# ACT and DVE follow the order of the source in the mixer of a hybrid encoder layer

## The chip, the core and the metric

The kernel runs on one core of a Trainium2 chip. The metric is the time of one execution in device microseconds. Five engines work side by side, each through its own queue of instructions: TensorE (PE, matrix products), VectorE (DVE) and ScalarE (ACT) for element-wise work, GpSimd (POOL), and SyncE (SP), which starts most transfers.

## What is computed

The reference is one encoder layer on 512 tokens of width 1024. All is in float32.

```
x = x + 0.5 * swiglu(rms_norm(x, ffn1_norm), ffn1_w_gate, ffn1_w_up, ffn1_w_down)
h = rms_norm(x, mix_norm)
qkv_a, z_a, a_a, b_a, qkv_b = split(h @ w_in)
o_a = gdn_mixer(qkv_a, z_a, a_a, b_a, conv_w, a_log, dt_bias, gdn_norm_w)
o_b = dilated_mixer(qkv_b, q_norm_w, k_norm_w, rel_bias)
x = x + concat(o_a, o_b) @ w_out
x = x + 0.5 * swiglu(rms_norm(x, ffn2_norm), ffn2_w_gate, ffn2_w_up, ffn2_w_down)
x = rms_norm(x, final_norm)
```

`gdn_mixer` is a gated delta rule in both directions, with 4 heads of 128: a centred convolution of width 5 over the tokens of q, k and v, a decay per head, and per chunk of 64 tokens the inverse of a triangular matrix, followed by a scan over the chunks. `dilated_mixer` is attention with 8 heads of 64, in three patterns of window and dilation.

## The kernel before

The stages are FFN1, mixer, output projection, FFN2 and a last norm. Tokens lie on the free axis, 512 to a tile, and channels on the 128 partitions. To get float32 results from faster products, each operand is split into a high half (a rounded copy) and a low half (the rest), and each product is made of three matmuls: high by high, high (weight) by low, low (weight) by high (`mm3`).

In the mixer the input projection is cut into units of 128 output channels, named by what they make: K0 to K3 and Q0 to Q3 (keys and queries of the delta rule), V0 to V3, Z0 to Z3 (the gate of its output), and Pa, Pb, v for the attention. A unit takes two weight chunks of 128x512, and a chunk is used by twelve matmuls. A chunk (`wrw`) is loaded by SP; `split` makes its high half on ACT and `sub` its low half on DVE (`wsp`). `wnext` hands out chunks and lets the next splits be traced, one chunk ahead.

After a K, Q or V unit `conv` multiplies the result `pc` by the norm factor R on DVE (`xp`), makes the first tap on ACT and four more taps on DVE (`kT`, `qT`, `vT`). The gates (`gt`, from `ab` and `abT`) are small operations of 128x32 on DVE with a few on ACT. `gram` makes for one head the squares on ACT, the products `pkk` and `pkq` on TensorE, and from them for both directions `itr` on DVE, a product on POOL and `M` on DVE, four each. `M` of all heads goes to DRAM and comes back as `MM` in another layout; `solve` copies it on DVE and runs 31 steps (`stp`, `ZZ`) on DVE. Attention tiles are `L`, `PT` and `ou`; `otok` holds the scan's output.

What sets the order: six generators trace the mixer's work, and `interleave` picks the next piece by planned costs and due times; ORDER lists the projection units. What is so traced is then put on the engines by a scheduler, which may choose another order within an engine. In the mixer TensorE is exempt: `PEQueue` ties each matmul behind the one traced before it while `te.fixed` holds.

Of the kernel before, what the change touches and what calls it, by code (L numbers as in the profile page):

```python
# [58 lines left out]
        return self._call(self.te.transpose, *a, **k)  # L59


def interleave(streams):


    due = {i: 0.0 for i in range(len(streams))}
    need, events, t = {}, {}, 0.0
    while due:
        for i in list(need):
            if need[i] in events:
                due[i] = max(due[i], events[need.pop(i)])  # L70
        live = [i for i in due if i not in need]
        now = [i for i in live if due[i] <= t]
        if not now:
            t = min(due[i] for i in live)
            continue
        i = now[0]
        y = next(streams[i], None)
        if y is None:
            del due[i]
        elif y[0] == "set":  # L80
            events[y[1]] = t + y[2]
        elif y[0] == "need":
            need[i] = y[1]
        else:
            t += y[0]
            due[i] = t + y[1]
# [2 lines left out]
@with_exitstack  # L89
def encoder_layer(ctx, tc, xT, gu1, dn1, win, wab, wo1, wo2, gu2, dn2, cols, relb, masks, onehot, lnc, sel, out):  # L90
    nc = tc.nc
    te, ve, se, gp, sy = PEQueue(tc, nc.tensor), nc.vector, nc.scalar, nc.gpsimd, nc.sync

    const = ctx.enter_context(tc.tile_pool(name="const", bufs=1))
    xp_ = ctx.enter_context(tc.tile_pool(name="xp", bufs=1))
# [9 lines left out]
    def pfl(name):  # L105
        return ps.tile([P, T], F32, tag="fl", name=name, bufs=2)
# [16 lines left out]
    def tmp(tag, name, n=T, dt=F32, bufs=2):  # L123
        return tp.tile([P, n], dt, tag=tag, name=name, bufs=bufs)
# [30 lines left out]
    def preload():  # L155
        with ExitStack() as es:
            for i in act["silu"][-8:]:
                es.enter_context(tc.issue_after(i.ins))
            act["pre"] = se.preload_act_table_set(LE)
        act["silu"] = []  # L160
# [76 lines left out]
    def rsq(o, src, n, tag="sq"):  # L237
        a = tmp(tag, "nw")
        w = o.shape[-1]
        a = a[:, 0:w]  # L240
        lx(o, src, AF.Ln, bias=eps, scale=1.0 / n)
        lx(o, o, AF.Exp, scale=-0.5)
        se.activation(a, o, AF.Square, scale=1.0 / math.sqrt(n))
        ve.scalar_tensor_tensor(out=a, in0=src, scalar=n * EPS, in1=a, op0=ALU.add, op1=ALU.mult)
        ve.scalar_tensor_tensor(out=o, in0=a, scalar=-3.0, in1=o, op0=ALU.add, op1=ALU.mult)

    class Norm:
        def __init__(self, ccol, lone=None, fast=False):
            self.acc = tmp("ssq", "ssq", bufs=1)
            self.c, self.lone, self.fast, self.tail = ccol, lone, fast, None  # L250
# [116 lines left out]
    with ExitStack() as mctx:  # L367
        mp = mctx.enter_context(tc.tile_pool(name="mp", bufs=1, reuse_waits="tile"))

        def mt(shape, name, tag=None, dt=F32, bufs=1):  # L370
            return mp.tile(shape, dt, name=name, tag=tag or name, bufs=bufs)
# [202 lines left out]
        def silu1(t):  # L574
            with tc.issue_after(act["dexp"].ins):
                silu(t, t)
# [91 lines left out]
        def norms():  # L668
            for pr in range(4):
                yield ("need", f"pair{pr}")  # L670
                if pr == 0:
                    yield ("need", "vsilu")
                if pr:
                    yield ("need", f"split{pr - 1}")
                for isq, t, sq in pend[pr]:
                    pn = pfl("pnb")
                    te.matmul(pn, lhsT=mk[:, M_BLK:M_BLK + P], rhs=sq, start=True, stop=True)
                    yield 0.86, 0.0
                    rs = tmp("g", "rsb")
                    n = mt([P, T], "qn" if isq else "kn")  # L680
                    rsq(rs, pn, 64.0)
                    ve.scalar_tensor_tensor(out=n[:, ::-1] if isq else n, in0=t,
                                            scalar=wqk[:, 0:1] if isq else wqk[:, 1:2], in1=rs, op0=ALU.mult,
                                            op1=ALU.mult)
                    qkn[isq] = n
                yield ("set", f"norm{pr}", NRG)
# [13 lines left out]
        def post_val(h, vT):  # L700
            pt = pflip("ptr")
            for c in range(NC):
                te.transpose(out=pt[:, c * P:(c + 1) * P], in_=vT[:, c * P:(c + 1) * P], identity=ident)
            for c in range(NC):
                se.mul(vtok[:, h, c, :], pt[:, c * P:(c + 1) * P], ivn[:, h * 4 + c:h * 4 + c + 1])

        def after():
            for i in range(8):
                yield ("need", f"post{i}")
                kind, h, t = posts[i]  # L710
                if kind == "V":
                    yield ("need", "solve" if h > 1 else "gram")
                    if h == 2:
                        yield ("need", f"post{i + 1}")
                        for n in range(2):
                            gin["taps", 10 + n]()
                            silu1(posts[i + n][2])
                        preload()
                        yield ("set", "vsilu", 0.0)
                        yield 0.0, VTP  # L720
                    post_val(h, t)
                else:
                    post_v(h, t)
                yield 0.43, VTS
                if kind == "v":
                    yield ("set", f"vb{h}", VBG)
                if sum(p[0] == "V" for p in posts[:i + 1]) == 4:
                    yield ("set", "vtok", VTG)
# [61 lines left out]
        def chain():  # L790
            for h in range(NH):
                yield ("need", f"gin{h}")
                yield from gram(h)
            ve.reciprocal(t16, ivn)
            ve.tensor_tensor(out=t16, in0=t16, in1=wk, op=ALU.mult)
            ve.tensor_tensor(out=ivn, in0=ivn, in1=t16, op=ALU.add)
            ve.tensor_scalar(out=ivn, in0=ivn, scalar1=0.5, scalar2=None, op0=ALU.mult)
            yield ("set", "gram", 1.0)
            yield from solve()
            yield ("set", "solve", SVG)  # L800
            yield from levels()
# [268 lines left out]
        def fin(pr):  # L1070
            oh_[4 + pr], ol_[4 + pr] = slot(f"xh{pr}", "oh", F32R), slot(f"xl{pr}", "ol", F32R)
            split(oh_[4 + pr], ol_[4 + pr], obs[pr])
# [132 lines left out]
        def fins():  # L1205
            yield ("need", "proj")
            for pr in range(4):
                yield ("need", f"close{pr}")
                fin(pr)
                if pr == 1:  # L1210
                    yield ("set", "fin", FNG)

        ss = [fins(), chain(), after(), norms(), att(), px()]
        interleave([ss[i] for i in PRI])
        te.fixed = False
        for d in range(NKT):
            x[d] = slot(f"x{d}")
# [130 lines left out]
```

## Time and profile before

| | |
|---|---|
| median of 3 runs | 1103.24 us (1103.19 to 1105.31) |
| the profiled execution's own time | 1104.93 us |
| its span | 1103.2 us |
| TensorE busy | 1067.6 us |
| DVE busy | 614.8 us |
| ACT busy | 443.4 us |
| POOL busy | 87.0 us |

The span is the time from the first to the last recorded instruction; the execution's own time has 1.7 us around it. FFN1 lasts to about 369 us, the mixer and output projection to 729, FFN2 to 1060.

### The profile page before, as it was taken

To read this page: it belongs to the slowest core of one execution; us is meant where nothing else is said; L and a number is where in the kernel's file an instruction comes from. 1 tells how busy PE (TensorE), PEld (TensorE's weight loads), DVE (VectorE), ACT (ScalarE), POOL (GpSimd) and SP (SyncE) were. 2 spreads that over 40 slices of the span, in tenths; PEclk is the share of its full clock that TensorE was granted. 3 is DMA by queue.
4 is the path that set the end of the run, shared out by engine and by line. 5 is a ranking of instruction groups with operands and counts; after the bars stand their busy time and mean duration, and the time that the engine had idled before them with its cause. 6 is when DMAs were issued, how large, how long until landed. Compare 5 with 4: busy or idle time off the path is not lost.

```text
span 1103.2 us, 14133 instructions
## 1 busy us (share of the span) xinstructions
PE 1067.6 (97%) x5394; PEld 879.2 (80%) x5394; DVE 614.8 (56%) x1113; ACT 443.4 (40%) x812; POOL 87.0 (8%) x123
## 2 busy tenths in 40 slices
PE   9999999999999999899999988999999999999996
PEld 7888888888888777778789766778888888888886
DVE  4544444443434398898787889675444444532223
ACT  6432222232232256434666666463222222332321
POOL 3000000000111222610000010000000000001001
PEclk9999999999999999989999999999999999999998
DMA  5332222234333133445422142232233323333332
GB/s 193 96 96 96 95 96 97 95 112 148 109 121 119 35 102 101 114 120 159 90 75 94 56 160 75 68 118 83 96 99 96 103 95 105 96 87 102 89 105 77
DMA packets 53235, 112.27 MB, mean 102 GB/s; under 512 B 17984, under 2 KB 20576, under 8 KB 53168
## 3 DMA queue, kind: packets, MB, share of 16 engines
q1 hardware_dynamic: 48976, 99.50, 29.3%
q0 software_dynamic: 2896, 10.25, 2.9%
q10 hardware_dynamic: 1296, 1.63, 0.5%
q8 instruction: 42, 0.69, 0.3%
q14 instruction: 25, 0.20, 0.1%
HBM read 102.39 MB, written 8.96 MB: 101 GB/s over the span
## 4 chain that ended last, share of the span: by engine, by line
PE 81%; DVE 11%; ACT 2%; issue 2%; DMA 1%; POOL 1%; DVEq 0%; SPq 0%; ACTq 0%; POOLq 0%
PE pg L52 22%; PE pd L52 22%; PE pu L52 22%; PE pc L50 3%; PE pd L50 2%; PE pqk L50 2%; DVE wsp L226 2%; PE ps L50 2%; PE pl L50 1%; PE pov L50 1%; PE pout L52 1%; PE pT L50 1%; DVE stp L842 1%; PE pS L50 1%; DMA wrw<-in_win 1%
## 5 line engine op out<-in xcount | busy, mean ns | idle before, releaser
L178 ACT CAST whi<-wraw 128x1024 fp32r<-128x1024 f32 (+1 forms) x138 | 137.5, 999 | 425.8 <-issue 167.6
L179 DVE TENSOR_TENSOR wlo<-wraw,whi 128x1024 fp32r<-128x1024 f32 (+1 forms) x138 | 161.1, 1168 | 135.5 <-ACT whi L178 131.2
L52 PE MATMUL pd<-hh,whi 128*128 128x512 f32 (+1 forms) x374 | 141.2, 378 | 0.0
L52 PE MATMUL pd<-hh,wlo 128*128 128x512 f32 (+1 forms) x374 | 140.9, 377 | 0.0
L52 PE MATMUL pd<-hl,whi 128*128 128x512 f32 (+1 forms) x374 | 140.8, 377 | 0.0
L52 PE MATMUL pg<-xh,whi 128*128 128x512 f32 x344 | 135.2, 393 | 0.7 <-ACT whi L178 0.5
L52 PE MATMUL pg<-xl,whi 128*128 128x512 f32 x344 | 135.0, 392 | 0.3 <-DVE xl L273 0.3
L52 PE MATMUL pg<-xh,wlo 128*128 128x512 f32 x344 | 134.6, 391 | 0.0
L52 PE MATMUL pu<-xh,wlo 128*128 128x512 f32 x344 | 133.8, 389 | 0.0
L52 PE MATMUL pu<-xh,whi 128*128 128x512 f32 x344 | 133.8, 389 | 0.0
L52 PE MATMUL pu<-xl,whi 128*128 128x512 f32 x344 | 133.8, 389 | 0.0
L316 DVE TENSOR_TENSOR u<-pu,R 128x512 f32<-128x512 f32 x44 | 30.4, 691 | 129.5 <-PE pu L52 129.5
L52 PEld LDWEIGHTS pd<-hl,whi 128*128 128x128 f32 x374 | 70.3, 188 | 13.1
L52 PEld LDWEIGHTS pd<-hh,whi 128*128 128x128 f32 x374 | 70.3, 188 | 12.9
L52 PEld LDWEIGHTS pd<-hh,wlo 128*128 128x128 f32 x374 | 70.3, 188 | 12.8
L314 DVE TENSOR_TENSOR g<-pg,R 128x512 f32<-128x512 f32 x44 | 30.4, 692 | 84.7 <-PE pg L52 84.6
L52 PEld LDWEIGHTS pg<-xh,whi 128*128 128x128 f32 x344 | 65.0, 189 | 15.0 <-ACT whi L178 1.2
L52 PEld LDWEIGHTS pg<-xl,whi 128*128 128x128 f32 x344 | 64.9, 189 | 14.9 <-DVE xl L273 1.1
L52 PEld LDWEIGHTS pg<-xh,wlo 128*128 128x128 f32 x344 | 64.8, 188 | 13.9 <-issue 0.2
L229 ACT CAST wsp<-wrw 128x512 fp32r<-128x512 f32 x76 | 47.2, 621 | 71.1 <-DMA wrw<-in_win 27.6
L52 PEld LDWEIGHTS pu<-xl,whi 128*128 128x128 f32 x344 | 64.6, 188 | 13.5
L52 PEld LDWEIGHTS pu<-xh,wlo 128*128 128x128 f32 x344 | 64.6, 188 | 13.3
(296 smaller groups left out, 1692.4 us busy)
## 6 DMA issues: line engine op xcount, KB each, us to landing
wraw<-in_gu SPq DMA_DIRECT2D x84, 512.0 KB, 3.5
wraw<-in_dn SPq DMA_DIRECT2D x32, 512.0 KB, 3.5
wrw<-in_win SPq DMA_DIRECT2D x56, 256.0 KB, 2.7
wraw<-in_dn SPq DMA_DIRECT2D x16, 384.0 KB, 3.1
wrw<-in_wo SPq DMA_DIRECT2D x16, 256.0 KB, 2.6
bw<-vec_d POOLq DMA_DIRECT2D x8, 448.0 KB, 4.0
x<-in_xT SPq DMA_DIRECT2D x8, 256.0 KB, 4.8
x_d<-x SPq DMA_DIRECT2D x8, 256.0 KB, 2.0
```

Of the source, the lines that this page charges most:

```text
L50: self.last = f(*a, **k)
L52: self.last = f(*a, **k)
L178: se.copy(hi[:, s], raw[:, s])
L179: ve.tensor_tensor(out=lo[:, s], in0=raw[:, s], in1=hi.bitcast(F32)[:, s], op=ALU.subtract)
L226: ve.tensor_tensor(out=o, in0=a, in1=b.bitcast(F32), op=ALU.subtract)
L229: se.copy(hi, src)
L314: ve.tensor_tensor(out=g, in0=pg, in1=R, op=ALU.mult)
L316: ve.tensor_tensor(out=u, in0=pu, in1=R, op=ALU.mult)
L842: ve.tensor_tensor(out=t, in0=Zs[:, rs_, s:s + 1].broadcast_to([P, ne, ncol]), in1=Mt[:, s:s + 1, s + 1:SB].broadcast_to([P, ne, ncol]), o ...
```

## The change

A class `Queue` wraps DVE and ACT as `PEQueue` wraps TensorE: while `fixed` holds, each instruction is tied behind the one traced before it on the same engine. A DMA that ACT starts is tied too, but nothing is tied behind it. `fixed` is set around the `interleave` call of the mixer. Computation and instructions are the same.

```
+class Queue:
+    def __init__(self, tc, eng):
+        self.tc, self.eng, self.fixed, self.last = tc, eng, False, None
+
+    def __getattr__(self, name):
+        f = getattr(self.eng, name)
+
+        def call(*a, **k):
+            if self.fixed and self.last is not None:
+                with self.tc.issue_after(self.last.ins):
+                    r = f(*a, **k)
+            else:
+                r = f(*a, **k)
+            if name != "dma_start":
+                self.last = r
+            return r
+        return call
...
-    te, ve, se, gp, sy = PEQueue(tc, nc.tensor), nc.vector, nc.scalar, nc.gpsimd, nc.sync
+    te, ve, se, gp, sy = PEQueue(tc, nc.tensor), Queue(tc, nc.vector), Queue(tc, nc.scalar), nc.gpsimd, nc.sync
...
         ss = [fins(), chain(), after(), norms(), att(), px()]
+        ve.fixed = se.fixed = True
         interleave([ss[i] for i in PRI])
+        ve.fixed = se.fixed = False
```

On TensorE the order of all instructions is the same. On DVE 706 rows of the order stand elsewhere, on ACT 411. In the rows below a row is one instruction (or several alike, x4) with its source line, operation, the tile it writes, the tiles it reads, and its size; the numbers behind names tell tiles apart. Rows of the wrapped engines have line 74 in the new kernel, that of the wrapper.

The first place is DVE after unit K0, where the gates begin. `wsp_2615` is the low half of Q0's second chunk, `wsp_2660` and `wsp_2725` are those of K1's two chunks, `xp_2648` belongs to K0 and `xp_2741` to Q0. Before:

```order
L428 TENSOR_TENSOR xp_2648<-pc_2583,R_80 128x512
L226 TENSOR_TENSOR wsp_2660<-wrw_2530,wsp_2660 128x512
L434 SCALAR_TENSOR_TENSOR kT_2544<-xp_2648,col_81,kT_2544 128x512 x2
L495 COPY abT_2551<-pabT_2676 128x64
L434 SCALAR_TENSOR_TENSOR kT_2544<-xp_2648,col_81,kT_2544 128x512
L504 TENSOR_TENSOR gt_2682<-abT_2551,col_81 128x32
```

In the new kernel:

```order
L74 TENSOR_TENSOR xp_2648<-pc_2583,R_80 128x512
L74 SCALAR_TENSOR_TENSOR kT_2544<-xp_2648,col_81,kT_2544 128x512 x4
L74 TENSOR_TENSOR ab_2657<-pab_2625,R_80 32x512
L74 TENSOR_TENSOR wsp_2615<-wrw_2530,wsp_2615 128x512
L74 COPY abT_2551<-pabT_2676 128x64
```

Behind 34 more rows of the gates, the new kernel goes on with:

```order
L74 TENSOR_TENSOR gl_2555<-g_2553,gh_2554 128x32
L74 TENSOR_TENSOR wsp_2660<-wrw_2530,wsp_2660 128x512
L74 TENSOR_TENSOR xp_2741<-pc_2659,R_80 128x512
L74 SCALAR_TENSOR_TENSOR qT_2543<-xp_2741,col_81,qT_2543 128x512 x4
L74 TENSOR_TENSOR wsp_2725<-wrw_2530,wsp_2725 128x512
```

`wsp_2615` stood ahead of `xp_2648` and stands now behind its four taps; `wsp_2660` stood ahead of the taps and stands now behind all of the gates.

The second place is DVE around head 1's gram block, with unit Q3 (`xp_3246`) and the chunks of V0 (`wsp_3153`, `wsp_3169`) and Pa0 (`wsp_3259`). Before:

```order
L226 TENSOR_TENSOR wsp_3153<-wrw_2530,wsp_3153 128x512
L226 TENSOR_TENSOR wsp_3169<-wrw_2530,wsp_3169 128x512
L428 TENSOR_TENSOR xp_3246<-pc_3152,R_80 128x512
L226 TENSOR_TENSOR wsp_3259<-wrw_2530,wsp_3259 128x512
L618 TENSOR_SCALAR wk_2567<-wk_2567 128x4
L619 RECIPROCAL n2k_2569<-wk_2567 128x4
L621 TENSOR_TENSOR c1_2560<-beta_2552,n2k_2569 128x2x4
L623 TENSOR_TENSOR bdec_2561<-c1_2560,cs_2558 128x2x4
L618 TENSOR_SCALAR wq_2568<-wq_2568 128x4
L638 TENSOR_TENSOR itr_3222<-pkq_3213,mk_83 128x512
L638 TENSOR_TENSOR itr_3229<-pkq_3213,mk_83 128x4x128
```

In the new kernel:

```order
L74 TENSOR_TENSOR bdec_2561<-c1_2560,cs_2558 128x2x4
L74 TENSOR_TENSOR itr_3222<-pkq_3213,mk_83 128x512
L74 SCALAR_TENSOR_TENSOR M_2547<-pkk_3212,c1_2560,M_2547 128x128 x4
L74 TENSOR_TENSOR itr_3229<-pkq_3213,mk_83 128x4x128
L74 SCALAR_TENSOR_TENSOR M_2547<-pkk_3212,c1_2560,M_2547 128x128 x4
L74 TENSOR_TENSOR xp_3246<-pc_3152,R_80 128x512
L74 SCALAR_TENSOR_TENSOR qT_2543<-xp_3246,col_81,qT_2543 128x512 x4
L74 TENSOR_TENSOR wsp_3169<-wrw_2530,wsp_3169 128x512
```

The two `itr` stood together ahead of the eight `M`, and each now stands ahead of its own four; `wsp_3169` moved from ahead of the block to behind it, `xp_3246` and its taps.

The third place is DVE where the solve begins. `MM_3444` is the matrix read back from DRAM, and `wsp_3363` the low half of V1's first chunk. Before (`wsp_3363` stands well ahead of the last `M`, and the copy of `MM` behind the splits of the units after V1):

```order
L643 SCALAR_TENSOR_TENSOR M_2547<-pkk_3302,c1_2560,M_2547 128x128 x8
L428 TENSOR_TENSOR xp_3352<-pc_3258,R_80 128x512
L226 TENSOR_TENSOR wsp_3363<-wrw_2530,wsp_3363 128x512
L226 TENSOR_TENSOR wsp_3454<-wrw_2530,wsp_3454 128x512
L434 SCALAR_TENSOR_TENSOR vT_3257<-xp_3352,col_81,vT_3257 128x512
```

Further behind on DVE, still before the change, the solve begins:

```order
L434 SCALAR_TENSOR_TENSOR vT_3257<-xp_3507,col_81,vT_3257 128x512
L226 TENSOR_TENSOR wsp_3542<-wrw_2530,wsp_3542 128x512
L584 TENSOR_TENSOR z_3575<-pz_3517,R_80 128x512
L832 COPY MM_3444<-MM_3444 64x1024
L842 TENSOR_TENSOR stp_3446<-ZZ_3445,MM_3444 128x31
```

In the new kernel:

```order
L74 SCALAR_TENSOR_TENSOR M_2547<-pkk_3406,c1_2560,M_2547 128x128 x4
L74 RECIPROCAL t16_2572<-ivn_2570 128x16
L74 TENSOR_TENSOR t16_2572<-t16_2572,wk_2567 128x16
L74 TENSOR_TENSOR ivn_2570<-ivn_2570,t16_2572 128x16
L74 TENSOR_SCALAR ivn_2570<-ivn_2570 128x16
L74 COPY MM_3444<-MM_3444 64x1024
L74 TENSOR_TENSOR stp_3446<-ZZ_3445,MM_3444 128x31
L74 TENSOR_TENSOR ZZ_3445<-ZZ_3445,stp_3446 128x31
L74 TENSOR_TENSOR wsp_3363<-wrw_2530,wsp_3363 128x512
L74 TENSOR_TENSOR qk_3470<-pqk_3362,R_80 128x512
L74 TENSOR_TENSOR wsp_3454<-wrw_2530,wsp_3454 128x512
```

The copy of `MM` moved ahead of `wsp_3363`, `wsp_3454` and what follows them.

## Rows read from the trace of the kernel before

**Rows 1.** The page: busy time and share of each engine; the chain that ended last.

```profile
PE 1067.6 (97%) x5394; PEld 879.2 (80%) x5394; DVE 614.8 (56%) x1113; ACT 443.4 (40%) x812; POOL 87.0 (8%) x123
...
PE 81%; DVE 11%; ACT 2%; issue 2%; DMA 1%; POOL 1%; DVEq 0%; SPq 0%; ACTq 0%; POOLq 0%
```

**Rows 2.** Windows: length, busy of PE, PEld, DVE, ACT, POOL; clock; DMA.

```profile
369.00:480.00 111.00, 102.50 (x482) 80.43 (x481) 90.25 (x197) 57.75 (x157) 40.33 (x64) 0.97 0.35 103
...
514.00:620.00 106.00, 101.66 (x971) 86.25 (x970) 78.20 (x187) 70.79 (x177) 3.82 (x7) 1.00 0.36 96
620.00:729.00 109.00, 98.32 (x530) 79.41 (x529) 88.25 (x200) 64.23 (x149) 8.18 (x14) 1.00 0.30 94
729.00:1060.00 331.00, 330.98 (x1456) 273.04 (x1456) 144.02 (x171) 106.05 (x134) 6.82 (x4) 1.00 0.31 98
```

**Rows 3.** Timeline between K0 and Q0: start, duration, engine, line, tiles, count.

```profile
380.42 0.69 DVE L428 TENSOR_TENSOR xp<-pc,R 128x512 f32<-128x512 f32 x1 [0.70 <-PE pc L50]
...
380.67 0.61 PE L50 MATMUL pc<-xh,wsp 128*128 128x512 f32 x2
...
381.07 0.69 DVE L226 TENSOR_TENSOR wsp<-wrw,wsp 128x512 fp32r<-128x512 f32 x1
...
381.14 0.72 ACT L430 ACTIVATE kT<-xp,col 128x512 f32<-128x512 f32 x1
381.35 0.61 PE L50 MATMUL pc<-xh,wsp 128*128 128x512 f32 x2
...
381.90 1.54 DVE L434 SCALAR_TENSOR_TENSOR kT<-xp,col,kT 128x512 f32<-128x512 f32 x2
```

**Rows 4.** Gates, groups of lines, 384 to 405: count, busy, mean ns, idle before.

```profile
L513 DVE TENSOR_TENSOR gt<-gt 128x32 f32<-128x32 f32 x8 | 1.4, 180 | 0.0
...
L164 ACT ACTIVATE gt<-gt 128x32 f32<-128x32 f32 x3 | 0.6, 224 | 2.0 <-DVE gt L519 1.5 <-DVE gt L505 0.5
```

**Rows 5.** Timeline of one gram block.

```profile
441.50 0.27 ACT L615 ACTIVATE sq<-ptk 128x128 f32<-128x128 f32 x1
...
443.78 1.29 DVE L638 TENSOR_TENSOR itr<-pkq,mk 128x512 f32<-128x512 f32 x2
...
444.55 1.29 POOL L640 TENSOR_TENSOR itr<-itr,M 128x512 f32<-128x512 f32 x1 [0.59 <-DVE itr L638]
...
445.88 1.12 DVE L643 SCALAR_TENSOR_TENSOR M<-pkk,c,M 128x128 f32<-128x128 f32 x4 [0.81 <-POOL itr L640]
```

**Rows 6.** Timeline of the last M; transfers of tile MM, first and last start.

```profile
466.39 2.15 DVE L643 SCALAR_TENSOR_TENSOR M<-pkk,c,M 128x128 f32<-128x128 f32 x8
...
L831 SPq DMA_DIRECT2D MM<-D x2: 466/500/535, 472.3 to 473.0; - x2
...
DMA to landing us min/median/max: 4.2/4.4/4.6
```

**Rows 7.** Timeline of TensorE after its longest wait; the window behind it.

```profile
469.39 0.77 PE L50 MATMUL pz<-xh,wsp 128*128 128x512 f32 x1 [4.58 <-DVE t L795]
...
469.40:474.40 5.00, 5.00 (x12) 3.96 (x13) 4.73 (x9) 1.70 (x3) 2.40 (x4) 0.50 0.49 141
```

**Rows 8.** Timeline around unit v1.

```profile
513.62 1.11 DVE L848 COPY ZZ<-ZZ 128x1024 f32<-128x1024 f32 x1
...
520.00 1.28 ACT L159 ACT_TABLE_LOAD   x1
...
521.87 0.63 PE L50 MATMUL pvb<-xh,wsp 128*128 128x512 f32 x2
...
526.92 0.50 PE L50 MATMUL pqk<-xh,wsp 128*128 128x512 f32 x1 [1.47 <-DVE qk L661]
```

**Rows 9.** Groups of DVE's lines, 514 to 729: the splits.

```profile
L226 DVE TENSOR_TENSOR wsp<-wrw,wsp 128x512 fp32r<-128x512 f32 x33 | 22.7, 686 | 10.4 <-ACT wsp L229 10.3
```

**Rows 10.** The page: DMA issues, count, KB each, us to landing.

```profile
wrw<-in_win SPq DMA_DIRECT2D x56, 256.0 KB, 2.7
```

## The prediction

> **What bounds the kernel now.** I read the page's shares first. TensorE is busy 97% of the span and carries 81% of the chain that ended last; DVE is busy 56% and ACT 40% [rows 1]. So the time is TensorE's work plus the gaps in it, and a change that touches only DVE and ACT can act on nothing but the gaps. The table of windows shows where gaps exist: TensorE idles 8.5 us of the 111 us from 369 to 480 (projections, gates, gram blocks), 4.3 and 10.7 us in the two windows from 514 to 729 (attention, scan, output), and nothing in FFN2 [rows 2]. The reader is to see two things there. Few gaps are left to close. And DVE is far from idle where the change acts: 90.25 of 111 us in the first of these windows, 88.25 of 109 in that from 620 to 729. An order that makes DVE wait has 21 us to spare in the first, if the waits fall well.
>
> The change leaves FFN1 and FFN2 alone (the switch is on only around the mixer), and TensorE's own order is the same before and after. What moves is the place of each DVE and ACT instruction among its neighbours. The one that matters most is the split of a weight chunk: ACT casts the high half, DVE subtracts the low half, and the third of the chunk's twelve matmuls needs the low half. Twelve matmuls take 2.7 us (three start 0.68 us apart, from 380.67 to 381.35) and the split takes 0.69 us of DVE [rows 3]. Before, the scheduler set splits ahead of their use, between taps: at 381.07 one runs ahead of all four taps of the same unit.
>
> **The change part by part.**
>
> *Conv handover.* In the traced order the low half of a unit's second chunk stands behind xp and the four taps of the unit before. That makes a loop: low half 0.69, the ten matmuls left of the chunk 2.3 and 0.4 until their result is there, xp 0.69, ACT's first product 0.72, four taps 4 x 0.77 = 3.1, next low half: 8.0 us [rows 3]. TensorE has 24 matmuls, 5.45 us, per unit, so each handover loses up to 2.55 us. Seven handovers have this form (K0 to Q0, Q0 to K1, K1 to Q1, Q1 to K3, K3 to Q2, K2 to Z0, V1 to Z3). Walking them in order, with what each had left, gives 2.8, 3.0, 2.0, 2.5, 2.2, 2.6, 2.3 = 17.4; Z0 to Q3 gives 1.4. The first low half of all, now behind FFN1's last x7, gives 1.2 more (two operations of DVE's size). Sum 20.0. Bounds: 8 (DVE work fits the gaps in half of them) to 24.
>
> *Gates.* Now 37 small DVE operations and three ACT calls stand in one block ahead of the low half of K1's first chunk. They take 37 x 0.2 = 7.4 us (0.18 by the row, and 0.02 between two) and 0.9 for ACT (0.6 by the row, and three hand-overs) [rows 4], then 0.69 for the split; Q0's second chunk covers 2.7: 6.3 us. Before, taps and splits stood between these operations. Bounds: 4 (the ACT calls overlap and half of DVE's rows run while Q0's chunk lasts) to 8 (nothing of K0's handover is left to cover it).
>
> *Gram blocks of heads 0 to 2.* One block is: squares on ACT from 441.50, itr on DVE from 443.78, POOL's product on itr 1.29, four M on DVE 1.12, and the last three once more for the other direction. The split for TensorE's next chunk stands behind it. In a strict order the second itr waits for the first four M, so DVE is twice held by POOL: 2.3 us of squares and small operations, then 0.77 + 1.29 + 0.04 + 1.12 twice, is 8.7 us [rows 5]. With the split 9.4; pkk and pkq on TensorE cover 1.8: 7.6. The three, by what else stands ahead, come to 6.0, 8.3 and 7.6 = 21.9. Bounds: 10 (the chunk before covers 2.7 each and the second POOL wait is overlapped) to 24.
>
> *The solve's matrix.* The low half of V1's first chunk now stands behind the copy of MM, and MM goes from SBUF to DRAM and back. In the trace the last M ends at 466.39 + 2.15 = 468.54; the second read is issued at 473.0 and lands 4.6 later, at 477.6: 9.1 us [rows 6]. The copy takes 1.1 (as the copy of ZZ, of the same size, in the next part), the first solve step two small operations of 0.2, the split 0.69. Behind a gram block of 8.7 that is 20.0 in all; pkk, pkq and Pa0's second chunk cover 4.5: 15.5. Before, this place costs TensorE 4.58 waiting and 2.3 at the half clock that follows (twelve matmuls take 5.00 there, granted clock 0.50, which is the 1.2 GHz level) [rows 7]; 6.9 of the 15.5 are thus no loss: 8.6. Queued behind the copy are V1's split, the qk eviction and Z3's splits. Bounds: 4 to 16.
>
> *v1.* The second chunk's low half stands behind ZZ's copy 1.11, eight taps 6.2, a silu and three calls of the norm on ACT (four at 0.7, as ACT's product above), a table load 1.28, then six norm operations of DVE, one eviction and the split (eight at 0.69): 16.9 us. TensorE had work from the copy's start, 513.62, to the second of the two matmuls of 521.87, at 522.10, the first of the chunk: 8.5. The stall is 8.4, less the 1.47 that TensorE already waits there at 526.92 [rows 8]: 6.9. Bounds: 2 to 9.
>
> *Attention, scan, output (530 to 729).* The rows move by three to six places only, but 33 splits of 0.69 [rows 9] and a few evictions go into line, and a block of sixteen otok rows comes ahead of an attention block. If only that block costs: 4. If every split costs its 0.69 and the evictions and otok rows theirs: 40. DVE is about as loaded here (74% and 81% of the two windows) as in the first window (81%), but the moves are small: I take 15, two thirds of the splits' 22.7.
>
> *Clock.* The trace has one long stall, and after it the granted clock is 0.50 for twelve matmuls, 2.3 us lost [rows 7]. Of the new stalls some five last longer than that one; the walk above has them following each other, some of them inside a half clock that hides behind the next wait. I take 3; bounds 0 to 15.
>
> *At nothing.* The wrapper adds no instruction. A chunk's load on SP's queue waits until an earlier chunk's split has freed its buffer, so the loads start later; one lands 2.7 us after its issue [rows 10], and the 8 us loop of a handover, in which two are needed, covers that. If it did not, each of the 22 units would wait up to 2.7 us more; nothing of the sort shows before, and the 40 of the upper bounds holds a part of it. ACT's casts of the high halves move too, but the low halves come later and decide. FFN2 takes its 331 us.
>
> Sum: 20.0 + 6.3 + 21.9 + 8.6 + 6.9 + 15 + 3 = 81.7. The profiled execution took 1104.93 us with a span of 1103.2; the median of the runs is 1103.24, 1.7 lower. On top of the median the change gives 1184.9, so I say 1185 (the profiled execution would be near 1187). The lower bounds add to 8 + 4 + 10 + 4 + 2 + 4 + 0 = 32 (1135), the upper to 24 + 8 + 24 + 16 + 9 + 40 + 15 = 136 (1239).
>
> **Rivals.**
>
> *Slower, but the waits hide* (about 1135). Speaking for it: DVE has 21 us free in the first window, and each wait delays TensorE only once, since the loops are not additive when TensorE is already late. The lower bounds then hold everywhere: +32. Against it: each handover is a closed loop through TensorE, so being late does not shorten it.
>
> *The clock falls in every stall* (about 1215). The kernel of before shows one: 4.6 us idle, then 0.50 for 5 us [rows 7]. If each of the eleven places with 2 us or more of stall costs about 2.3 us in the same way, that is 25 to 30 us in place of 3. For it: the row. Against it: the 15 us of gaps in the two windows from 514 to 729 came with a granted clock of 1.00 in both [rows 2]. The Trainium skill, TensorE: Matmul & The Clock Gate, section "What's actually happening", says that the default state is throttled and that activity releases the throttle; the row of 0.50 agrees, the gaps at 1.00 show that not every gap counts, and by the rule read strictly this rival would be the forecast.
>
> *The strict order is better* (about 1096). The scheduler of before has one bad place: wsp and the qk eviction wait behind eight M, TensorE idles 4.58 us and then loses 2.3 [rows 7]. In the traced order the M of one head come earlier, two blocks of four; if that brought the splits there in time, the 6.9 us would be saved. It decides if the handovers and blocks ahead of it cost less than 6.9 us in all, that is if DVE never stands still at the head of its queue. Against it: in the order of after V1's split is behind the copy of MM, which can't begin before 9.1 us after the last M [rows 6], so that place gets worse, not better.
>
> *Nothing happens* (1103). It would hold if the scheduler already kept the traced order. It does not: 706 of DVE's rows and 411 of ACT's stand elsewhere, and the blocks shown ahead are among them.
>
> **How the numbers follow.** The forecast 0.72, its own range 1150 to 1210; the waits hide 0.13; the clock falls everywhere 0.10; the strict order better 0.03; nothing 0.02. To leave out no more than 2 in 10, the range goes from 1135 to 1225: it takes in the sum of lower bounds, and most of the clock rival. A measurement of this kernel tells about 0.2%, 2.2 us, from no change. Faster 0.03, same 0.02, slower 0.95.
>
> **What would show it.** TensorE's count and order of matmuls the same, its busy time nearly so; its gaps up from 8.5 to about 60 us in the stretch that was 369 to 480 and 514 to 530. Waits of TensorE put down to DVE's wsp splits at every unit, 2 to 3 us each, with one of 6 behind the gates, three of 6 to 8 at the gram blocks and one near 15 at V1. POOL's itr as what DVE waits for, twice a head, 1.3 us each. DVE waiting some 9 us for the MM read. FFN1 and FFN2 unchanged in length. I am wrong if the gaps are there but shorter than the loops say (a split is then earlier than I read it), if the stretch from 530 on grows by more than 40 us, or if the granted clock outside the mixer changes.

## The result and the profile after

The changed kernel takes 1242.23 us (median of 4 runs, 1240.38 to 1243.23) against 1103.83 for the kernel before: a ratio of 1.1228, 95% interval 1.1184 to 1.1272, or 138 us more. The forecast was 1185 with a range up to 1225; the direction was right, the size was not.

The page of the changed kernel, busy time and the chain that ended last (against [rows 1]):

```profile
PE 1119.2 (90%) x5394; PEld 910.8 (73%) x5394; DVE 620.1 (50%) x1113; ACT 440.6 (36%) x812; POOL 86.3 (7%) x123
...
PE 68%; DVE 17%; ACT 8%; issue 4%; DMA 1%; POOL 1%; DVEq 0%; SPq 0%; ACTq 0%; POOLq 0%
```

The counts are the same, and DVE and ACT do the same work in nearly the same time. TensorE went from 35.6 us idle (1103.2 - 1067.6) to 121.6, which is 86 more, and is busy 52 us longer with the same 5394 matmuls. The chain now runs for a quarter of the span through DVE and ACT (13% before).

The windows show where. The mixer is cut at one instruction, the first matmul of unit Pa1: at 526.9 before, at 600.9 after. The kernel before, from the mixer's start to Pa1 and from Pa1 to FFN2 (columns as in [rows 2]):

```profile
369.00:526.90 157.90, 147.87 (x682) 116.65 (x680) 132.99 (x355) 78.69 (x197) 40.86 (x65) 0.98 0.40 113
526.90:729.10 202.20, 188.63 (x1449) 157.26 (x1450) 157.78 (x374) 126.44 (x308) 12.01 (x21) 1.00 0.29 87
```

The same two stretches of the changed kernel, and FFN2:

```profile
369.00:600.90 231.90, 170.09 (x680) 128.55 (x679) 138.72 (x358) 81.31 (x204) 39.74 (x65) 0.85 0.30 82
600.90:866.10 265.20, 218.04 (x1450) 176.34 (x1450) 159.68 (x373) 124.10 (x305) 11.99 (x21) 0.88 0.21 65
866.10:1197.00 330.90, 330.75 (x1456) 272.85 (x1455) 143.81 (x170) 105.94 (x134) 6.82 (x4) 1.00 0.31 97
```

The stretch up to Pa1 (called the projections below) grows by 74.0 us: TensorE idles 61.8 instead of 10.0 and is busy 22.2 longer, at a granted clock of 0.85. The stretch behind it (attention, scan and output) grows by 63.0: idle 47.2 instead of 13.6, busy 29.4 longer, at 0.88. FFN2 is unchanged.

Three places of the first stretch, in the timeline of the changed kernel. First DVE and TensorE between K0 and K1 (against [rows 3, 4]):

```profile
381.10 0.69 DVE L74 TENSOR_TENSOR xp<-pc,R 128x512 f32<-128x512 f32 x1 [3.73 <-PE pc L50]
382.59 3.11 DVE L74 SCALAR_TENSOR_TENSOR kT<-xp,col,kT 128x512 f32<-128x512 f32 x4 [0.79 <-ACT kT L74]
...
386.22 0.67 DVE L74 TENSOR_TENSOR wsp<-wrw,wsp 128x512 fp32r<-128x512 f32 x1
...
395.79 0.19 DVE L74 TENSOR_TENSOR gl<-g,gh 128x32 fp32r<-128x32 f32 x1 [0.20 <-ACT gh L74]
396.30 0.69 DVE L74 TENSOR_TENSOR wsp<-wrw,wsp 128x512 fp32r<-128x512 f32 x1 [0.33 <-ACT wsp L74]
...
396.32 0.80 PE L50 MATMUL pc<-xh,wsp 128*128 128x512 f32 x1 [4.57 <-ACT wsp L74]
```

xp, ACT's product, four taps, split: the loop is there with the durations of the prediction. The gates then hold DVE from 387.4 to 395.8, 8.4 us, where the prediction had 8.3. But what TensorE waits for at K1 is the chunk's first matmul, which needs only the high half, ACT's cast.

Then head 3's gram block and the matrix (against [rows 5, 6, 7]):

```profile
505.99 1.12 DVE L74 SCALAR_TENSOR_TENSOR M<-pkk,c,M 128x128 f32<-128x128 f32 x4 [1.40 <-POOL itr L661]
507.03 0.68 DVE L74 TENSOR_TENSOR itr<-pkq,mk 128x512 f32<-128x512 f32 x1
509.62 1.12 DVE L74 SCALAR_TENSOR_TENSOR M<-pkk,c,M 128x128 f32<-128x128 f32 x4 [1.92 <-POOL itr L661]
...
517.77 1.03 DVE L74 COPY MM<-MM 64x1024 f32<-64x1024 f32 x1 [5.84 <-DMA MM<-D]
...
519.17 0.68 DVE L74 TENSOR_TENSOR wsp<-wrw,wsp 128x512 fp32r<-128x512 f32 x1
...
519.90 1.22 PE L50 MATMUL pc<-xh,wsp 128*128 128x512 f32 x2 [13.29 <-DVE wsp L74]
```

DVE waits twice for POOL and once for the read of MM, with V1's split behind it, and TensorE idles 13.29 us at the chunk's third matmul, the first that needs the low half. Behind the wait two matmuls take 1.22 us, twice the 0.62 of full clock.

And unit v1, DVE, ACT's last two rows ahead of the wait's end, and TensorE (against [rows 8]):

```profile
575.85 1.12 DVE L74 COPY ZZ<-ZZ 128x1024 f32<-128x1024 f32 x1
576.87 6.14 DVE L74 SCALAR_TENSOR_TENSOR vT<-xp,col,vT 128x512 f32<-128x512 f32 x8
587.03 0.69 DVE L74 SCALAR_TENSOR_TENSOR nw<-pnb,nw 128x512 f32<-128x512 f32 x1 [4.02 <-ACT nw L74]
...
591.37 0.69 DVE L74 SCALAR_TENSOR_TENSOR nw<-pnb,nw 128x512 f32<-128x512 f32 x1 [2.14 <-ACT nw L74]
...
595.38 0.69 DVE L74 TENSOR_TENSOR wsp<-wrw,wsp 128x512 fp32r<-128x512 f32 x1 [1.20 <-ACT wsp L74]
...
594.21 0.63 ACT L74 ACTIVATE sq<-qk 128x512 f32<-128x512 f32 x1 [2.87 <-DVE qk L74]
594.74 0.60 ACT L74 CAST wsp<-wrw 128x512 fp32r<-128x512 f32 x1
...
595.40 0.80 PE L50 MATMUL pvb<-xh,wsp 128*128 128x512 f32 x1 [12.64 <-ACT wsp L74]
```

Here too it is the first matmul of the chunk that waits, for the high half: ACT's cast stands behind a square that waits for DVE. TensorE's longest groups of waits in the projections (us in total, times, longest):

```profile
PE pc L50 <- DVE wsp L74: 17.7, 4, 13.3
PE pvb L50 <- ACT wsp L74: 12.6, 1, 12.6
PE pc L50 <- ACT wsp L74: 12.1, 3, 7.3
PE pdc L50 <- DVE gb L74: 6.4, 2, 5.4
PE pz L50 <- ACT wsp L74: 4.6, 2, 3.2
PE pqk L50 <- DVE wsp L74: 3.8, 1, 3.8
```

The high halves (12.6, 12.1 and 4.6) make 29.3 us of them and the low halves 21.5; `gb`, an operand of the decays, makes 6.4.

In the second stretch no single wait stands out. Groups of lines on ACT and DVE from 601 to 866 (busy, mean ns, idle before):

```profile
L74 ACT ACTIVATE L<-L,mx 128x512 f32<-128x512 f32 x32 | 23.1, 723 | 69.2 <-DVE mx L74 69.2
...
L74 DVE TENSOR_TENSOR PT<-pT,PT 128x512 fp32r<-128x512 f32 x32 | 22.0, 686 | 20.8 <-ACT PT L74 20.8
...
L74 DVE TENSOR_TENSOR ou<-pov,tl 64x256 f32<-64x256 f32 x16 | 6.7, 417 | 17.8 <-ACT tl L74 17.7
```

The same three waits before, from 530 to 729:

```profile
ACT L L164 <- DVE mx L1091: 7.8, 9, 1.7
...
DVE ou L1125 <- ACT tl L1124: 3.9, 3, 2.2
...
DVE PT L226 <- ACT PT L1105: 1.4, 5, 0.5
```

Attention's exp waits at the head of ACT's queue for DVE's maximum in every one of its 32 calls, 69.2 us in all; before it was 7.8. DVE waits at its head 20.8 us for ACT's half of PT (1.4 before) and 17.7 for tl (3.9 before). One such wait, with the row behind it:

```profile
693.16 0.39 PE L50 MATMUL pS<-KA,ql 128*128 128x512 f32 x1
...
695.43 0.69 DVE L74 TENSOR_TENSOR PT<-pT,PT 128x512 fp32r<-128x512 f32 x1 [3.44 <-ACT PT L74]
...
696.04 0.68 DVE L74 CUSTOM_DVE_ANT_0 L<-pS,bw 128x512 f32<-128x512 f32 x1
```

DVE stands 3.44 us for ACT's cast. The next row, L of another block, has its pS from 693.55 on and can't pass.

### The profile page after: what moved, and what is told of

It reads as the page before. It is cut to its first block, busy times and chain, and to the rows that moved or that the text cites. A ratio compares the mean times of both kernels' runs of the same rounds, so it can differ in the third digit from the quotient of the medians.

```text
span 1240.8 us, 14097 instructions
## 1 busy us (share of the span) xinstructions
PE 1119.2 (90%) x5394; PEld 910.8 (73%) x5394; DVE 620.1 (50%) x1113; ACT 440.6 (36%) x812; POOL 86.3 (7%) x123
## 4 chain that ended last, share of the span: by engine, by line
PE 68%; DVE 17%; ACT 8%; issue 4%; DMA 1%; POOL 1%; DVEq 0%; SPq 0%; ACTq 0%; POOLq 0%
PE pd L52 19%; PE pg L52 19%; PE pu L52 19%; PE pc L50 3%; DVE wsp L74 2%; DVE PT L74 1%; PE pd L50 1%; DVE L L74 1%; PE pl L50 1%; ACT L L74 1%; DVE vT L74 1%; ACT wsp L74 1%; ACT vn L74 1%; POOL itr L661 1%; DVE kT L74 1%
## 5 line engine op out<-in xcount | busy, mean ns | idle before, releaser
L50 PE MATMUL pc<-xh,wsp 128*128 128x512 f32 x192 | 74.6, 457 | 29.8 <-DVE wsp L74 17.7
L52 PEld LDWEIGHTS pu<-xh,wlo 128*128 128x128 f32 x344 | 64.5, 188 | 13.5
L52 PEld LDWEIGHTS pu<-xh,whi 128*128 128x128 f32 x344 | 64.6, 188 | 13.4
```

Source lines behind the costliest of these rows:

```text
L50: self.last = f(*a, **k)
L52: self.last = f(*a, **k)
```

## The experiments

The table gives for each profiled execution how much later than in the kernel before TensorE starts the first matmul of unit K1, of V1, of Pa1, and of FFN2. Times count from TensorE's first matmul of a kernel. Kernels that are alike up to a unit differ there by some 2 us to either side (V1: 44.5 to 48.7), and the medians of the kernel before, taken again beside the experiments, go from 1104.9 to 1107.5 us; smaller differences than these say nothing.

| kernel | K1 | V1 | Pa1 | FFN2 | of that behind Pa1 | median time |
|---|---|---|---|---|---|---|
| changed | 9.5 | 47.0 | 74.0 | 137.0 | 63.0 | 1242.2 |
| DVE alone fixed | 5.6 | 44.1 | 67.5 | 114.2 | 46.7 | 1218.5 |
| ACT alone fixed | 8.9 | 27.4 | 37.9 | 65.5 | 27.6 | 1169.7 |
| fixed up to Pa1 | 10.0 | 46.6 | 76.8 | 82.9 | 6.1 | 1185.3 |
| fixed from Pa1 on | 0.0 | -0.3 | -0.9 | 68.0 | 68.9 | 1171.8 |
| splits free | 6.1 | 25.1 | 44.9 | 104.6 | 59.7 | 1210.0 |
| solve free | 10.4 | 47.9 | 68.1 | 128.6 | 60.5 | 1232.9 |
| gates, gram, solve free | 5.0 | 32.6 | 46.7 | 107.4 | 60.7 | 1213.7 |
| filler in projections | 11.0 | 64.5 | 77.7 | 138.5 | 60.8 | 1243.8 |
| filler in attention | 10.4 | 48.0 | 75.1 | 139.4 | 64.3 | 1245.0 |
| exp free | 11.2 | 48.7 | 76.6 | 122.8 | 46.2 | 1224.2 |
| attention free | 9.7 | 47.9 | 75.8 | 99.7 | 23.9 | 1205.4 |
| attention and norms free | 9.1 | 45.7 | 72.5 | 80.0 | 7.5 | 1184.9 |
| attention and scan free | 9.8 | 44.5 | 74.5 | 78.5 | 4.0 | 1184.5 |
| attention, splits, output free | 4.8 | 23.9 | 43.6 | 71.8 | 28.2 | 1176.5 |
| all named groups free | 0.3 | 4.4 | 10.5 | 34.2 | 23.7 | 1139.4 |

"Free" means that these instructions are issued without the tie, so that the scheduler places them; the rest stays tied.

**Which engine, which stage.** One engine alone is fixed:

```
-        ve.fixed = se.fixed = True
+        ve.fixed = True
```

> Only DVE keeps the order of the source in the mixer; ACT is left to the scheduler. Theory A (DVE's order is the cause: the low halves of the weight chunks and the copies stand behind taps, gates, M and MM): nearly the whole of the 138 us stays, 1220 to 1245 us. Rival B (ACT is where the attention stage is lost, since its exp waited 69 us for DVE's mx with its casts behind it): the 74 us of the projections stay, most of the 64 us of attention, scan and output go, 1175 to 1195 us.

1218.51 us (1217.95 to 1219.07). Just under theory A and far above rival B: DVE's order alone makes 67.5 of the 74 us of the projections and 46.7 of the 63 behind them.

The same with `se.fixed` in the place of `ve.fixed`:

> Only ACT keeps the order of the source in the mixer; DVE is left to the scheduler. Theory A (DVE's order is the cause): 1105 to 1125 us. Rival B (ACT's order alone loses most of what attention, scan and output lost): 1145 to 1170 us.

1169.67 us (1168.86 to 1170.47): theory A missed, and the time lies in rival B's band for another reason than B's: ACT's order alone costs 66 us, but 38 of them in the projections and only 28 behind. The two engines' losses are not separate shares: they add to more than the whole. TensorE's waits say why. With DVE alone fixed its longest ones in the projections are at the same places as with both; those at K1, V0 and v1 are now for the low half instead of the high:

```profile
PE pc L50 <- DVE wsp L74: 28.2, 6, 13.5
PE pvb L50 <- DVE wsp L74: 12.0, 1, 12.0
```

The wait at v1 is 12.0 us there and 12.6 with both: holding either half of a chunk back is enough.

The switch is taken back, or first set, at Pa1 in the list of units:

```
             for u in ORDER.split():
+                if u == "Pa1":
+                    ve.fixed = se.fixed = False
```

> Both engines keep the order of the source only up to the last projection unit but five (Pa1), then the scheduler is free. If the losses of the two stages add, as the lag of TensorE by stage says (74 us at the start of Pa1): 1175 to 1180 us. Rival (a late start of the second stage is caught up there, TensorE idling 15 us in it before): 1160 to 1170 us. By the prediction's own sum (63.7 of gaps, 3 of clock): 1168 to 1171.

1185.28 us (1182.88 to 1187.68), above all three bands: 76.8 late at Pa1, and 6.1 more behind it. Nothing is caught up.

> Both engines keep the order of the source only from unit Pa1 on: attention, scan, output. If the losses of the stages add: 64 us, 1165 to 1170 us. By the prediction's sum (15 us, bounds 4 to 40): 1107 to 1143 us. Rival (most of the loss of this stage comes from what the first stage pushed into it): below 1125 us.

1171.78 us (1170.5 to 1173.07), just above the first band. The late stage loses its whole 68.9 us by itself, with a punctual start. This is the run that speaks against the prediction's term of 15 and its upper bound of 40.

**The projections.** Only the splits of the weight chunks are free:

```
-            split(ready[i][:, 0:T], ready[i][:, T:2 * T], fetched.pop(0))
+            hi, lo, src = ready[i][:, 0:T], ready[i][:, T:2 * T], fetched.pop(0)
+            nc.scalar.copy(hi, src)
+            nc.vector.tensor_tensor(out=lo, in0=src, in1=hi.bitcast(F32), op=ALU.subtract)
```

> Only the splits of the mixer's weight chunks (the cast on ACT, the subtraction on DVE) are taken out of the fixed order; all else on both engines keeps it. By the prediction's sum all that the projections lose is lost at splits that stand behind other work: the lag at the start of Pa1 falls from 74 us to 10 to 20, and the time to 1175 to 1190 us. Rival (DVE and ACT are held at the head of their queues anyway, and the wait moves to xp, gb and the evictions): the lag at Pa1 stays above 45, the time above 1210 us.

1209.99 us (1209.43 to 1210.55), lag at Pa1 44.9: at the rival's edge, far from the prediction's sum. TensorE's waits in that run's projections:

```profile
PE pz L50 <- DVE qk L74: 19.0, 1, 19.0
PE pqk L50 <- DVE qk L74: 8.6, 1, 8.6
PE pdc L50 <- DVE gb L74: 7.1, 3, 5.2
```

With the splits out of the line TensorE waits at the same places for the next one in it: the eviction of qk, which stands behind the copy of MM like the split, and gb behind a gram block.

Only the solve's instructions on DVE are free (`nc.vector` in the place of `ve` in `solve`, up to the copy of ZZ):

> Only the solve's instructions on DVE (copy of MM, 31 steps, copy of ZZ) are taken out of the fixed order. Theory (V1's low half waits for the copy of MM, and v1's stands behind the copy of ZZ): the lag that grows by 11 us from V1 to Z3 and by some of the 14 from v1 to Pa1 is gone, 10 to 18 us less in all, 1224 to 1232 us. Rival (the gram block of head 3 alone holds V1's split long enough, and the solve's later start costs as much further on): within 4 us of 1242.

1232.9 us (1232.17 to 1233.62). The lag at Pa1 falls by 5.9 and at FFN2 by 8.4: the solve's copies cost something, a little less than the least that the theory gave them.

The gates, gram blocks and the solve are free on both engines, the decays on ACT only; their rows on DVE (`gb`) keep the tie in this edit, against what the expectation says:

> The gates, decays, gram blocks and the solve are taken out of the fixed order on both engines; convs, splits, evictions, norms, scan and attention keep it. By the prediction's sum the handovers (20) and v1 (7) are left of the projections: lag at the start of Pa1 20 to 30 instead of 74, time 1190 to 1200 us. Rival (the splits behind the taps lose more than the sum says, the blocks less): lag at Pa1 above 40, time above 1208.

1213.65 us (1212.82 to 1214.47), lag at Pa1 46.7: the rival. The blocks gave back 27 us of the 37 that the prediction's terms for them make (6.3 + 21.9 + 8.6). TensorE's waits in that run's projections:

```profile
PE pvb L50 <- ACT wsp L74: 11.5, 1, 11.5
PE pc L50 <- DVE wsp L74: 10.2, 7, 2.3
```

The handovers show here: seven waits for the low half, 10.2 us in all and 2.3 the longest; and v1's wait of 11.5, which no gate or gram block touches, remains. They do not show alone: chunks of pc and pz wait another 9.4 us for the high half, and `gb` makes 6.5.

**The clock.** TensorE gets matmuls whose result nobody reads, 220 in all, ahead of twelve chunks, with 50 ahead of V1's and 48 ahead of v1's second:

```
+        fill = {3: 8, 4: 16, 7: 6, 9: 8, 11: 8, 13: 16, 15: 8, 19: 28, 20: 14, 22: 50, 25: 10, 41: 48}
+        seen = [0]
...
             for u in range(2):
                 wh, wl = wnext()
+                zz = pat("zz") if seen[0] in fill else None
+                for _ in range(fill.get(seen[0], 0)):
+                    te.matmul(zz, lhsT=xh[0][:, 0:P], rhs=xh[0], start=True, stop=True)
+                seen[0] += 1
```

> As the changed kernel, with 220 matmuls more whose result nobody reads, put ahead of twelve weight chunks so that TensorE works through most of its waits of the projections (50 us of work at 0.227 each). Theory C (the half clock behind each wait is a cost of its own, some 22 of the 74 us that the projections lose): the granted clock there goes to 1.00 and the time falls by 10 to 22 us, to 1220 to 1232. Rival D (the loops through DVE and ACT set the pace, and a slow TensorE only fills its own waits): the clock goes to 1.00 and the time stays within 5 us of 1242, or rises by what filler stands outside of a wait.

1243.82 us (1243.7 to 1243.95), in rival D's band, though the clock did not go to 1.00. The window of the projections in that run, its longest wait, TensorE behind V1's wait, and the window behind v1's wait; last, the same window of the changed kernel:

```profile
369.00:604.60 235.60, 208.00 (x903) 160.62 (x902) 138.41 (x358) 81.30 (x204) 39.86 (x65) 0.95 0.29 81
...
PE zz L50 <- ACT ktok L74: 9.8, 1, 9.8
...
526.09 0.73 PE L50 MATMUL pc<-xh,wsp 128*128 128x512 f32 x2 [1.92 <-DVE wsp L74]
...
599.40:605.00 5.60, 5.53 (x18) 4.26 (x19) 1.56 (x3) 3.22 (x11) 0.00 (x0) 0.70 0.32 97
...
595.40:601.00 5.60, 5.60 (x17) 4.46 (x18) 1.36 (x2) 3.14 (x10) 0.00 (x0) 0.57 0.29 94
```

The clock is 0.95 instead of 0.85, and the stretch takes 235.6 us instead of 231.9. Up to V0 the run speaks for D alone: V0 starts 31.6 us late, in the changed kernel 30.8, so the next wait took up what a slow TensorE had lost. From there on it is no clean test. The filler ahead of V0's second chunk first waits 9.8 us for the bank that it writes, and V1's third matmul, where the long wait ends, comes 6.2 us later than in the changed kernel. Behind that wait the clock was full this time: two matmuls took 0.73 us instead of 1.22, and at Z3 3.8 of the 6.2 are left, which stay to Pa1. So at V1 the half clock does cost some 2.4 us, and the filler's own delay hides the gain. Behind v1's wait the clock was low in both runs, and what it costs there is not tested.

The same in attention, fourteen matmuls behind each block of pov in the idle half of its bank:

```
-                pv = pov("pov")[:, 0:256]
+                pvt = pov("pov")
+                pv = pvt[:, 0:256]
...
+                for _ in range(14):
+                    te.matmul(pvt[:, 256:512], lhsT=vb[h][:, 3, :], rhs=PTh[:, 3, :], start=True, stop=True)
```

> As the changed kernel, with fourteen matmuls of 256 columns behind each of attention's sixteen blocks of pov, into the idle half of its bank, that nobody reads: about 27 us of TensorE's work at full clock (0.12 each, half of a 512-column one) in a stage in which it waits 47 us and is granted 0.88. Theory C (in this stage the half clock costs time of its own, up to the 31 us by which TensorE's busy time grew): the clock rises towards 1.00 and the time falls by 8 to 25 us. Rival D (as in the projections, DVE and ACT set the pace): the time stays within 5 us of 1242, or rises by up to 15 where the filler stands outside of a wait.

1244.98 us (1244.81 to 1245.15): rival D again, and a weaker test, since the clock rose only from 0.88 to 0.93 and what the filler costs by itself is not separated. The window from Pa1 to FFN2 in that run:

```profile
601.50:868.00 266.50, 231.70 (x1675) 196.51 (x1674) 159.28 (x372) 124.14 (x306) 11.95 (x21) 0.93 0.20 65
```

**Attention, scan, output.** Only the exp of attention is free:

```
-                lx(L, L, AF.Exp, bias=mx[:, 32 + n:33 + n], accum_out=den[:, n:n + 1])
+                with tc.issue_after(act["pre"].ins):
+                    nc.scalar.activation(L, L, AF.Exp, bias=mx[:, 32 + n:33 + n], accum_out=den[:, n:n + 1])
```

> Only attention's exp on ACT (32 instructions) is taken out of the fixed order. Theory (it stands at the head of ACT's queue for DVE's mx, 69 us in all where it was 8 before, with the casts of PT, tl and the splits behind it): the 63 us that attention, scan and output lose fall to 25 to 40, the time to 1205 to 1220 us. Rival (DVE's own order holds this stage, as the run with DVE alone lost 47 us there): the time falls by less than 10 us, above 1232.

1224.22 us (1220.79 to 1227.65): 18 us less; the stage still loses 46.2, as much as with DVE alone fixed (46.7). By the number the exp may be all that ACT's order adds to DVE's there, which is less than the theory said; that it is the same loss is not shown.

Attention's L, mx, exp, PT, tl and ou are free:

> Attention's exp, L, mx, the casts and subtractions of PT, tl and ou are taken out of the fixed order on both engines; all else keeps it. Theory (in this stage DVE stands 21 us at PT's low half for ACT's high half, 18 at ou for tl, and ACT 69 at exp for mx, each with other work behind): of the 63 us that the stage loses 10 to 25 are left, time 1190 to 1205 us. Rival (freeing only exp, which gave 18 us, was all that there is; scan, norms and splits hold the rest): above 1218.

1205.38 us (1205.08 to 1205.68). The stage loses 23.9 instead of 63.0, inside the theory's 10 to 25; the time is at the edge of what it gave. DVE's waits at the head of its queue in that run, from Pa1 on:

```profile
DVE PT L250 <- ACT PT L1137: 4.5, 4, 3.4
...
DVE ou L1157 <- ACT tl L1156: 3.5, 4, 2.2
```

They were 20.8 and 17.7. Three runs then freed one group each on top of this one, to find the other 24 us. The norms of q and k and their splits (`norms`, `split_pair`, `post_v`):

> On top of attention's instructions, the norms of q and k, their splits into high and low halves, and the values' splits are taken out of the fixed order. If these hold the rest of the loss of the stage (DVE still waits for ACT at nw, vb and KA there): 8 to 15 us below the run with attention's alone (1205), 1190 to 1197. If they don't: within 3 us of 1205.

1184.9 us (1184.89 to 1184.91): the stage loses 7.5.

The levels, the scan and o_post:

> On top of attention's instructions, the levels of the inverse, the scan and o_post (with goh and the otok block) are taken out of the fixed order. TensorE still waits 6 us for goh and 5 for vn and st there with attention's alone free: if that is where the rest is lost, 8 to 15 us below 1205, 1190 to 1197. If not: within 3 us of 1205.

1184.48 us (1183.82 to 1185.13): the stage loses 4.0. Each of the two groups took more than the expected 8 to 15. They cannot both hold 16 to 20 of 24 us. A reading that fits is that the two are tied to each other, and that freeing either one loosens both; no run frees them together or either one without attention.

The weight splits and the output projection:

> On top of attention's instructions, the splits of all the mixer's weight chunks and the instructions of the output projection are taken out of the fixed order. From the run that freed the splits alone, the projections lose 29 us less; if the rest of the last stage hangs on splits too, another 5 to 15: 1161 to 1171 us. If not: 1174 to 1180.

1176.45 us (1176.23 to 1176.68): the projections' gain alone; the stage still loses 28.2. The output side is not where it goes.

**All together.** The splits, gates, decays, gram, solve and attention's instructions are free:

> All groups named so far are taken out of the fixed order together: splits of the weight chunks, gates, decays, gram blocks, solve, and attention's L, exp, PT, tl, ou. Convs, evictions, norms, scan, levels and output keep it. Theory (the loss is in these groups, each at the head of a queue in front of another): 1110 to 1130 us. Rival (any fixed chain through the mixer makes the free groups wait for their fixed neighbours): above 1150 us.

1139.37 us (1139.15 to 1139.6): of 138 us, 103 are gone. The time lies between the theory's 1130 and the rival's 1150; `gb` on DVE stayed tied here too. In the projections 10.5 are left. TensorE's longest waits in that run's mixer are for what stayed tied:

```profile
PE pqk L50 <- DVE qk L74: 7.4, 1, 7.4
PE pd L50 <- ACT goh L74: 6.6, 2, 4.0
PE pz L50 <- DVE qk L74: 5.6, 1, 5.6
```

No run came below the kernel before.

## Why the prediction was wrong in size

**What bounds the kernel: right.** TensorE's gaps in the mixer grew, and FFN2 and the counts are as before. Only TensorE's busy time, expected to stay nearly the same, rose by 52 us at the lower clock.

**Handovers, gates, gram blocks, matrix: right in sum, in part by luck.** The terms up to K1 (first low half 1.2, first handover 2.8, gates 6.3) make 10.3; K1 comes 9.5 late. From there to Z3's first matmul the lag grows to 58.0 in the changed kernel; the prediction's terms up to there make 54.5 (all 63.7 but V1's handover 2.3 and v1's 6.9). Two waits are where the text put them: 13.29 us at V1 against 15.5, 4.57 behind the gates against 6.3. But the parts do not hold one by one. With gates, gram and solve free only 27 of their 37 us came back, and TensorE was still 34.6 us late at v1, where the handovers were to make 20. Waits for splits at every unit, 2 to 3 us each, were not seen: at handovers they show at Q1, K3, Z0 and Z3 alone, 1.3 to 3.2 us. The 7.26 us in V0, next behind V1's, are for the high half, and the 5.4 at `gb` had no term. That "the low halves come later and decide" was wrong: the high halves made 29.3 us of TensorE's waits and the low halves 21.5. ACT's casts were put at nothing; beside DVE's order, ACT's adds 6.5 us up to Pa1 (74.0 against 67.5) and 16.3 behind it (63.0 against 46.7). The run with the splits free shows one more limit: the split is not the only one in the line, so the loss goes to whoever stands behind the same head.

**v1: right place, half the size.** 6.9 us were forecast; with V1's handover of 2.3 the lag should grow by 9.2 from Z3 to Pa1, and it grew by 16.0. The time from the copy of ZZ to the end of the split is 20.2 us (575.85 to 596.07) and not 16.9: DVE waits twice for the norm's chain on ACT, 4.02 and 2.14, where the prediction counted one chain, and 1.20 for the cast of the high half. TensorE had work for 6.9 us behind the copy's start (its wait begins at 582.76), not 8.5. Behind the wait the chunk takes 5.55 us up to Pa1 (595.40 to 600.95) where before it took 3.35 (522.10 to 526.92, less the 1.47 of waiting): 2.2 us of half clock.

**Clock: in the projections the size of the term fits and the rival's does not; in attention it is open.** The granted clock fell in most stretches of the mixer, as the rival said, and TensorE's busy time rose by 52 us. But up to V0 a clock of 0.95 in place of 0.88 (369 to 480) bought nothing: there the next wait is set by DVE and ACT, and a slow TensorE only fills it. To add the clock's whole loss to the waits counts these microseconds twice. It is not nothing everywhere. TensorE's own matmuls are a part of the handover loop, and behind V1's wait full clock gave 2.4 us; behind v1's the half clock takes 2.2 that no run removed. Together that is 4.6, near the 3 that was taken and far from the rival's 25 to 30. The Trainium skill (TensorE: Matmul & The Clock Gate, section "What's actually happening") says that activity releases the throttle. The filler's 0.95 agrees. For attention, what the clock costs is open: it could be raised only to 0.93.

**Attention, scan, output: the step that failed.** "The rows move by three to six places only ... but the moves are small: I take 15", with 40 as the upper bound; it is 63.0, and 68.9 when only this stage is fixed. That this stretch grows by more than 40 us was among the prediction's own signs of being wrong. Of the 55 us by which the sum missed TensorE's lateness at FFN2 (137.0 against 81.7), this term makes 48 and v1 most of the rest. Distance in the order was the wrong measure, and the splits' 0.69 the wrong price. A row that moves by three places costs nothing if its operands are there, and costs the whole wait if it now stands at the head of a queue without them. Here each attention block is a relay between the two engines: maximum on DVE, exp on ACT, cast of PT on ACT, its low half on DVE, tl on ACT, ou on DVE. In the traced order a station's row comes as soon as its supplier's was traced on the other engine, so the queue stops there until the supplier is done, with rows of other blocks behind it that can be ready, as L at 696.04 was. ACT's 69.2 us at exp and DVE's 38.5 at PT and ou are these waits (TensorE does not lose all of them), and freeing these instructions took 39 of the 63 us away. The rest hangs on the scan and the norms, which are tied as well; how it divides between them is open, since freeing either one removes most of it.

**The forecast's range.** The upper bounds of the parts summed to 1239, 3 below the result. The range ended at 1225, which leaves out that the parts reach their bounds together; attention went past its bound (63.0 against 40), and so did v1 (14.0 from v1 to Pa1 against 9). Three sums of the prediction are off, and none decides: the handover loop's terms make 7.9 us and not 8.0, three of the seven handovers stand above the 2.55 that it gives as the most, and the clock rival's 25 to 30 us in place of 3 make 1207 to 1212 and not 1215.

## What to carry to other kernels

An order that was planned for one engine is not for that reason right for its helpers: on DVE and ACT it put waits for another engine ahead of work that was ready. To price a fixed order, walk each queue for rows whose operands come from another engine, stage by stage, and ask what ready work stands behind them. The sum of such waits shows where to look and is not the loss (107.7 us at exp, PT and ou in a stage that lost 63.0); small moves in the order were no sign of a small loss here. And before a slow clock of TensorE is priced, see at each place whether TensorE is the one that is waited for: filler raised the clock here and gave no time back up to V0, while behind V1's long wait full clock gave 2.4 us.

## What the runs showed of the hardware beyond what was expected

The granted clock was 0.85 and 0.88 on average in the two stretches of the mixer, in which TensorE stood 61.8 and 47.2 us, in waits of up to 13.29 and 5.2 us. In the kernel before it was 1.00 in the second stretch, where TensorE stood 13.6 us in waits of up to 2.5. Behind the 13.29 us wait, two matmuls took 1.22 us in place of 0.62, the 1.2 GHz level; in the filler run, where TensorE worked ahead of V1's third matmul and stood only 1.92 us, they took 0.73.
